# Wide values, a closing tile by halves, sample scaling in PSUM, and late forms behind the last row: five edits to a two-layer encoder kernel

## The chip, the cores and the metric

The kernel runs on one core of a Trainium2 chip. The metric is the device time of one execution in microseconds (us); lower is better. Before the change the median of three runs is 2803.09 us (2794.26 to 2809.61).

## The reference, cut to what matters

Two layers, each a token mixer (attention) and a channel mixer (a gated MLP with a convolution of width 3 over positions), for 1024 prompt tokens and 8 samples of 16 tokens, width 1024, 16 heads of 64, MLP width 2816, all in fp32. Every sub-layer is modulated by a condition c (one vector for the prompt, one for each sample) and closed by a layer norm:

```python
for l in range(2):
    sh_m, sc_m, g_m, sh_f, sc_f, g_f = split(silu(c) @ w_ada[l] + b_ada[l], 6)
    h = x * (1 + sc_m) + sh_m
    if l == 0:                       # mixer A: window of 3 chunks, 4 K/V heads
        q, k, v = split(h @ w_qkv_a)
    else:                            # mixer B: band of 9 chunks, 16 K/V heads
        q = h @ w_q_b                # k_b, v_b: see below
    mix = attention(q, k, v) @ w_o
    x = layer_norm(ALPHA * x + (1 + g_m) * mix, ln_g[l, 0], ln_b[l, 0])
    h = x * (1 + sc_f) + sh_f
    a, g = split(causal_conv3(h @ w_up[l]), 2)
    x = layer_norm(ALPHA * x + (1 + g_f) * ((gelu(g) * a) @ w_down[l]), ln_g[l, 1], ln_b[l, 1])
    if l == 0:                       # one K/V for mixer B, from its own modulation
        sh_kv, sc_kv = split(silu(c) @ w_ada_kv + b_ada_kv, 2)
        k_b, v_b = split((x * (1 + sc_kv) + sh_kv) @ w_kv_b, 2)
return x, ...                        # and the new K, V and convolution rows
```

## The kernel before, in words

The tokens lie in nine tiles of 128: tiles 0 to 7 are the prompt, tile 8 holds the samples. A tile's modulated rows stand transposed in H (`H[:, t, part, chunk, :]`). Every matrix is split into a high and a low part (`split`: a cast, L165, on ScalarE, and a subtraction, L176, on DVE or POOL), and each product is three matmuls, low x high, high x low, high x high. `wload` brings a piece of weights through a staging buffer `ws` (DMA issued by SP, L180) and splits it into a pair of slots, `wh` and `wl`.

Each layer goes through `attention`, `out_proj`, `up_phase` and `down_phase`. The code is written as one stream, and a scheduler that simulates the program's time on each engine sets the order of each engine's instructions; dependencies between tiles of memory are found by it, and `issue_after` adds a constraint by hand (what stands inside it comes after the named instruction).

- In layer 1's `attention`, K and V for mixer B are projected first. `vproj` takes V in four quarters of 256 columns: per quarter 9 tiles, per tile 24 matmuls (`mmX`, L395), whose result ScalarE casts (L444), DVE subtracts (L445) and SP stores as `vH` (L446); half of the tiles are copied by ScalarE once more for the output (L450). Quarter 0 comes before K (`kproj`, L383, with `rescale` on POOL), quarters 1 to 3 behind it. Then `qload(0)` brings the first block of query weights, and `load_hm` reloads the nine tiles that modulate into H for the queries (from `hmD`), modulates them (L907 on ScalarE; tile 8 by `sample_affine`) and splits them. H of a tile is free for this when V's last matmul on that tile has run.
- `sample_affine` scales and shifts tile 8, where each sample has its own vectors: per chunk of 128 columns one multiplication (L1006) and one addition (L1007) on DVE.
- `out_proj` computes per tile two halves of 512 columns into PSUM (`product`), multiplies by the gate in PSUM (L1045), adds the residual (L1046; `lasthalf` keeps the last of these), and `norm_tail` does the layer norm (L940 statistics, L971 normalisation), transposes on TensorE (L977) and modulates (L989 on ScalarE; tile 8 by `sample_affine`). Then `forms` builds sums and differences of blocks of the result, which the up-projection multiplies in seven products (P1 to P7) instead of eight. Forms are built for two token halves, q = 0 and q = 1. Those of q = 1 are the late forms: apart from P1 and P2 they are ordered after `lasthalf`.
- `up_phase` runs the seven products of both halves (L1225), with copies out of PSUM (L1243, L1254) and additions on DVE.
- `down_phase` takes three groups of three tiles (matmuls L1376, two halves `hf` for each tile). A tile's result is multiplied by the gate (`drain`, L1390) and, in layer 1, summed with the residual (L1401, with the row's sum accumulated) and normed by `norm_last`, which for tiles in VT takes two DVE operations (L958, L959) and for others ScalarE, POOL and DVE (L962 to L964), and is stored (L965). The last tile of the program is tile 8, not in VT.

Of the kernel before, what the change touches and what calls it, by code (L numbers as in the profile page):

```python
# [19 lines left out]
NFF = 22  # L20
# [73 lines left out]
class Trunk:  # L94
# [334 lines left out]

    def vproj(self, l, q, banks, tmp):  # L430
        nc = self.nc
        w = [self.wload(self.I[("wv0", "wv1")[l]][q, i], el="pv"[l == 0]) for i in range(2)]
        o0 = (896, 512)[l]
        cs = slice(q * 256, q * 256 + 256)
        for t in LV:
            ps = self.bank(banks.next())
            self.mmX(ps, t * 128, w, 4, 256)
            hl, v = tmp.next()
            v = v[:, 0:256]
            ts = slice(t * 128, t * 128 + 128)  # L440
            if t < 8:
                h4 = hl[:, 0:512].rearrange("p (h i d) -> p h i d", i=2, d=64)
                p3 = ps[:, 0:256].rearrange("p (h d) -> p h d", d=64)
                nc.scalar.copy(h4[:, :, 0, :], p3)  # L444
                nc.vector.tensor_sub(h4[:, :, 1, :], p3, h4[:, :, 0, :].bitcast(F32))  # L445
                nc.sync.dma_start(  # L446
                    self.vH[l][ts, 4 * q : 4 * q + 4, :], hl[:, 0:512].bitcast(F32).rearrange("p (h d) -> p h d", d=128)
                )
            if t * 128 >= o0:
                nc.scalar.copy(v, ps[:, 0:256])  # L450
                nc.sync.dma_start(self.O[("va", "vb")[l]][t * 128 - o0 : t * 128 - o0 + 128, cs], v)
            if t == 8:
                nc.sync.dma_start(self.vS[l][:, cs], v)


    def attention(self, l, wk):
# [67 lines left out]
        with ExitStack() as es:  # L524
            if l == 0:
                es.enter_context(self.tc.issue_after(self.lastx))
            self.vproj(l, 0, kvb, kvt)
        if l == 0:
            self.skew(0)
        else:  # L530
            zr = ka.ring(2, 1024)
            for c in range(8):
                self.kproj(1, c, self.wload(I["wk1"][c]), kvb, kvt)
                self.rescale(c, zr)
            self.rescale(8, zr)
            for q in range(1, 4):
                self.vproj(1, q, kvb, kvt)
            self.wring = Ring(self.wslots[0:2])
            qload(0)
            self.load_hm(Ring([pall[:, i * 1024 : i * 1024 + 1024] for i in range(3)]), self.affine(4, (8, 9), 1))  # L540
# [357 lines left out]
    def load_hm(self, ring, aff):  # L898
        nc, lead = self.nc, self.lastact
        G, B = aff  # L900
        for t in range(NT):
# [3 lines left out]
            if t < 8:  # L905
                for c in range(8):
                    nc.scalar.activation(s3[:, c, :], s3[:, c, :], AF.Identity, bias=B[:, c, 0:1], scale=G[:, c, 0:1])  # L907
            else:
                self.sample_affine(s3, s3, G, B, 0, 8, "v")
            with ExitStack() as es:  # L910
# [25 lines left out]
    def stats(self, x):  # L936
# [9 lines left out]
        return mv[:, 0:1], r  # L946

    def norm_last(self, t, x, s, ydst, junk):

# [17 lines left out]
    def norm_tail(self, t, x, xdst, aff, tb, h3, save=False):  # L967

        nc = self.nc
        mean, r = self.stats(x)  # L970
        nc.vector.tensor_scalar(x, x, mean, r, op0=ALU.subtract, op1=ALU.mult)  # L971
        sl = slice(t * 128, t * 128 + 128)
        G, B = aff
        for hf in range(2):
# [23 lines left out]

    def sample_affine(self, dst, src, G, B, c0, nc_, e):
        E = self.eng(e)  # L1000
        d4 = dst.rearrange("p c (s q) -> p c s q", q=16)
        s4 = src.rearrange("p c (s q) -> p c s q", q=16)
        for c in range(nc_):
            g = G[:, c0 + c, 1:9].unsqueeze(2).to_broadcast([128, 8, 16])
            b = B[:, c0 + c, 1:9].unsqueeze(2).to_broadcast([128, 8, 16])
            E.tensor_mul(d4[:, c], s4[:, c], g)  # L1006
            E.tensor_add(d4[:, c], d4[:, c], b)  # L1007

# [6 lines left out]
    def out_proj(self, l, xsrc, xdst, aff):  # L1015
# [26 lines left out]
        def add(t, x, hf, ps):  # L1042
            cs = slice(hf * 512, hf * 512 + 512)
            gate = self.gateP if t < 8 else self.gateS
            nc.vector.tensor_mul(ps, ps, gate[:, cs])  # L1045
            st = nc.vector.scalar_tensor_tensor(x[:, cs], x[:, cs], ALPHA, ps, op0=ALU.mult, op1=ALU.add)  # L1046
            self.lasthalf = st.ins

# [105 lines left out]
    def forms(self, q, hb, e, i):  # L1154
# [196 lines left out]
    def down_phase(self, l, xsrc, xdst, affs):  # L1351
# [19 lines left out]

        def mm(w, h, t, i, j):
            for hf in range(2):
                ps = self.bank(2 * i + hf)
# [61 lines left out]
        for g, ts in enumerate(GRP):  # L1436
# [16 lines left out]
            wh = [load(g, j) for j in range(NFF - nt, NFF)]  # L1453
            for i, t in enumerate(ts):
                for k, (w, h) in enumerate(wh):
                    mm(w, h, t, i, NFF - nt + k)
                row = rows.next()
                drain(i, t, row)
# [82 lines left out]
def layout(x):  # L1541
# [36 lines left out]
    z["wk1"] = cols(g["w_kv_b"][:, :D])  # L1578
    z["wv1"] = quarters(g["w_kv_b"][:, D:])
    z["wq1"] = cols(g["w_q_b"][0])  # L1580
# [58 lines left out]
```

## Time and profile before

| what | us |
|---|---|
| median of 3 runs | 2803.09 |
| the profiled execution | 2800.65 |
| its span in the trace | 2798.5 |
| TensorE matmuls busy | 2700.2 (96%) |
| DVE busy | 1665.2 (60%) |
| ScalarE busy | 1408.9 (50%) |
| POOL busy | 1056.7 (38%) |

The granted TensorE clock is 0.988 over the whole span. A matmul's busy time is modelled and includes its drain, so the 96% is a measure of how seldom TensorE waits, not of its rate. With so little waiting, an edit can act in two ways: it makes a stretch of matmuls itself shorter, or it shortens one of the few stretches in which TensorE stands. These are read from busy times by stage.

### The profile page before, as it was taken

The page shows a single profiled execution, that of the slowest core. Times are in us where ns is not written, and L with a number is a line of the kernel's source. Part 1 is how long each engine was busy: PE and PEld are TensorE (multiplying, and loading weights), DVE is VectorE, ACT ScalarE, POOL GpSimd, SP SyncE. Part 2 cuts the span into 40 slices and gives each one's busy share as a digit, 9 for nine tenths or more (in the row PEclk, how much of TensorE's full clock was granted, in tenths as well). Part 3 has the DMA queues.
Part 4 walks back from the last instruction along what each step waited for, and adds up shares of the span by engine and source line. Part 5 has one row for each costly group of instructions (what it writes and reads, how often), then busy time and mean ns, then how long its engine had stood idle before and what let it go on. Part 6 is the DMA issues. An engine that isn't in the chain of part 4 may idle for free.

```text
span 2798.5 us, 48858 instructions
## 1 busy us (share of the span) xinstructions
PE 2700.2 (96%) x18086; PEld 2415.9 (86%) x18086; DVE 1665.2 (60%) x3830; ACT 1408.9 (50%) x3012; POOL 1056.7 (38%) x1086
## 2 busy tenths in 40 slices
PE   8999889999999999999999999989899999999998
PEld 5887768999999998888999888867799999998886
DVE  4465757765555566766212677775966555567774
ACT  3465744544444444545425666662555445555441
POOL 1122337676566630001541121141877666640000
PEclk9999999999999999999999999999999999999999
DMA  9655443244444457865975456684222222238661
GB/s 331 193 155 164 124 140 113 97 139 138 155 134 128 146 158 266 310 215 182 303 249 177 113 150 185 168 250 132 99 89 74 78 83 75 76 104 290 232 209 71
DMA packets 215870, 454.47 MB, mean 162 GB/s; under 512 B 39280, under 2 KB 115264, under 8 KB 215632
## 3 DMA queue, kind: packets, MB, share of 16 engines
q1 hardware_dynamic: 215632, 451.35, 50.1%
q8 instruction: 143, 2.34, 0.3%
q14 instruction: 95, 0.78, 0.1%
HBM read 359.40 MB, written 101.30 MB: 165 GB/s over the span
## 4 chain that ended last, share of the span: by engine, by line
PE 77%; DVE 8%; DMA 7%; issue 4%; ACT 3%; POOL 1%; SPq 1%; POOLq 0%; ACTq 0%; DVEq 0%
PE PS L1225 34%; PE PS L1376 17%; PE PS L383 9%; PE PS L395 7%; DMA F<-in_adaw_dram 3%; PE PS L678 2%; PE PS L318 2%; PE PS L659 2%; PE PS L633 1%; DMA ws<-in_wo_dram 1%; DVE F L599 1%; PE PS L636 1%; DVE x1att L176 1%; PE PS L977 1%; PE PS L799 1%
## 5 line engine op out<-in xcount | busy, mean ns | idle before, releaser
L176 POOL TENSOR_TENSOR wl<-ws,wh 128x512 fp32r<-128x512 f32 (+1 forms) x217 | 324.2, 1497 | 649.3 <-ACT wh L165 628.3
L1279 DVE SCALAR_TENSOR_TENSOR PS<-F,PS 128x512 f32<-128x512 f32 (+2 forms) x704 | 349.1, 516 | 143.5 <-ACT PS L1286 63.6
L165 ACT CAST wh<-ws 128x512 fp32r<-128x512 f32 (+1 forms) x321 | 245.2, 769 | 313.6 <-PE PS L1376 99.3
L1225 PE MATMUL PS<-HX,wh 128*128 128x288 f32 x2616 | 401.0, 297 | 0.0
L1225 PEld LDWEIGHTS PS<-HX,wh 128*128 128x128 f32 x2616 | 364.4, 189 | 8.2 <-issue 8.2
L1376 PE MATMUL PS<-wh,HX 128*128 128x512 f32 x1164 | 361.7, 389 | 0.8 <-DVE HX L176 0.8
L1376 PEld LDWEIGHTS PS<-wh,HX 128*128 128x128 f32 x1164 | 218.4, 188 | 46.1 <-DVE HX L176 1.3
L1225 PE MATMUL PS<-HX,wl 128*128 128x288 f32 x1536 | 254.6, 297 | 0.2 <-ACT F L1254 0.2
L383 PE MATMUL PS<-HX,wh 128*128 128x384 f32 x1248 | 245.9, 340 | 0.0
L1376 PE MATMUL PS<-wl,HX 128*128 128x512 f32 x582 | 226.7, 390 | 0.6 <-DVE wl L176 0.6
L1225 PEld LDWEIGHTS PS<-HX,wl 128*128 128x128 f32 x1536 | 220.5, 189 | 7.1 <-issue 5.8
L383 PEld LDWEIGHTS PS<-HX,wh 128*128 128x128 f32 x1248 | 217.3, 189 | 5.4 <-issue 3.1
L1225 PE MATMUL PS<-x1att,wh 128*128 128x288 f32 x1168 | 181.9, 298 | 2.9 <-DVE x1att L176 1.3
L1286 ACT ACTIVATE PS<-F 128x512 f32<-128x512 f32 x176 | 138.1, 785 | 76.3 <-DVE F L1258 64.9
L1225 PEld LDWEIGHTS PS<-x1att,wh 128*128 128x128 f32 x1168 | 163.9, 189 | 8.9 <-issue 4.9
L395 PE MATMUL PS<-wh,HX 128*128 128x256 f32 (+1 forms) x936 | 168.4, 310 | 0.8 <-DVE C L599 0.8
L165 ACT CAST HX<-F 128x384 fp32r<-128x384 f32 (+3 forms) x232 | 136.6, 605 | 62.7 <-PE PS L1376 10.2
L717 POOL TENSOR_TENSOR F<-F,gatt 64x512 f32<-64x512 f32 x62 | 79.5, 1282 | 234.8 <-DVE F L690 181.5
L176 DVE TENSOR_TENSOR HX<-F,HX 128x384 fp32r<-128x384 f32 (+2 forms) x188 | 133.3, 719 | 37.2 <-ACT HX L165 33.6
L1376 PE MATMUL PS<-HX 128*128 128x512 f32 x630 | 145.1, 389 | 0.0
L395 PEld LDWEIGHTS PS<-wh,HX 128*128 128x128 f32 x936 | 133.8, 191 | 10.3 <-issue 1.5
L383 PE MATMUL PS<-HX,wl 128*128 128x384 f32 x624 | 130.3, 348 | 10.1 <-DVE HX L167 4.8
(244 smaller groups left out, 5486.2 us busy)
## 6 DMA issues: line engine op xcount, KB each, us to landing
F<-in_adaw_dram SPq DMA_DIRECT2D x112, 512.0 KB
ws<-in_wup_dram SPq DMA_DIRECT2D x92, 512.0 KB
ws<-in_wdn_dram SPq DMA_DIRECT2D x88, 512.0 KB
actD<-F SPq DMA_DIRECT2D x44, 576.0 KB
F<-actD SPq DMA_DIRECT2D x132, 192.0 KB
F<-in_wdn_dram SPq DMA_DIRECT2D x44, 512.0 KB
x1att<-kH SPq DMA_DIRECT2D x60, 256.0 KB
xd<-F SPq DMA_DIRECT2D x27, 512.0 KB
```

Source lines behind the costliest of these rows:

```text
L165: self.lastact = nc.scalar.copy(out, in_).ins
L176: self.eng(el).tensor_sub(lo, src, hi.bitcast(F32))
L318: mm = nc.tensor.matmul(ps[32 * j : 32 * j + 32, hf * 256 : hf * 256 + 256], self.cT[:, k * 32 : k * 32 + 32], w[n][:, j * 256 : j * 256 + ...
L383: self.nc.tensor.matmul(out, w[a][:, k * 128 : k * 128 + 128], self.Hx(p, k, s0, n), start=i == 0, stop=i == 23)
L395: self.nc.tensor.matmul(out[:, 0:n], H[:, t0 // 128, p, j * kn + k, :], w[a][:, k * n : k * n + n], start=i == 0, stop=i == 23,)
L659: nc.tensor.transpose(t[:, m * 128 : m * 128 + 128], p[:, (kt - k0) * 128 : (kt - k0) * 128 + 128], self.ident)
L678: nc.tensor.matmul(ob[:, i0 * 128 : i0 * 128 + w], vst[a][:, kt, :], pp[:, m1 : m1 + w], start=cnt == 0, stop=cnt == 2 * len(order) - 1, s ...
L717: self.eng("v" if last else "p").tensor_mul(on[r, q], on[r, q], rb[r, :])
L1225: nc.tensor.matmul(out, w[f][a][:, k * 128 : k * 128 + 128], x[:, k, :], start=start and i == 0, stop=i == 11, skip_group_check=True,)
L1279: nc.vector.scalar_tensor_tensor(o, v, w(i), o, op0=ALU.mult, op1=ALU.add)
L1286: nc.scalar.activation(yp, u[:, bl, 2:258], AF.Identity, bias=w(3), scale=w(2))
L1376: nc.tensor.matmul(ps, h[p][:, i * 128 : i * 128 + 128], w[q][:, hf * 512 : hf * 512 + 512], start=j == 0 and k == 0, stop=j == NFF - 1 an ...
```

## The change

Five things are done.

1. `vproj` takes its source, first column, width and destination as arguments. In layer 1, quarters 0 and 1 stay; columns 512 to 1023 are one half, 9 x 24 matmuls of 512 columns, with weights from a new array `wv1h` (four pieces of 128x1024). The weights of quarter 1 and of the half go to spare places in X1 and to weight slots 2 and 3, not through the ring `wring`; the half's evacuation ring has three buffers.
2. `sample_affine` is two operations per call over all its chunks: in `out_proj` a multiplication in place in PSUM and an addition from PSUM to SBUF, each 128x512; elsewhere the product goes to the destination first, as before.
3. The late forms are ordered after `lastnorm`, the normalisation of the last tile (L971, L1000 after), in place of `lasthalf`.
4. The program's last tile goes through a new function `close`: all matmuls of half 0, then all of half 1, with the gate's multiplication and the sum per half; the row's sum is put together; the Square on ScalarE runs beside the first closing operation on DVE; the second one and the store are done per half.
5. With these, the scheduler's order changes.

```diff
-    def vproj(self, l, q, banks, tmp):
+    def vproj(self, l, src, c0, n, banks, tmp, dst=None):
         nc = self.nc
-        w = [self.wload(self.I[("wv0", "wv1")[l]][q, i], el="pv"[l == 0]) for i in range(2)]
+        kn = 1024 // n
+        w = [self.wload(src[i], el="vp"[l], dst=dst and dst[i]) for i in range(8 // kn)]
...
-            self.mmX(ps, t * 128, w, 4, 256)
+            self.mmX(ps, t * 128, w, kn, n)
...
-            for q in range(1, 4):
-                self.vproj(1, q, kvb, kvt)
+            vt = [(self.X2[:, i * 1024 : i * 1024 + 1024], self.F[:, i * 512 : i * 512 + 512]) for i in range(3)]
+            spare = [tuple(self.X1[:, o + i : o + i + 1024] for i in (0, 1024)) for o in (0, 2048, 5120, 7168)]
+            spare += [self.wslots[2], (self.wslots[3][0], self.X1[:, 4096:5120])]
+            self.vproj(1, I["wv1"][1], 256, 256, kvb, kvt, spare[0:2])
+            self.vproj(1, I["wv1h"], 512, 512, kvb, Ring(vt), spare[2:6])
             self.wring = Ring(self.wslots[0:2])
             qload(0)
...
+    def close(self, t, row, x, ydst, product, junk):
+        nc = self.nc
+        part, rr = self.sm.next(), self.sm.next()
+        s, v, r = part[:, 0:1], rr[:, 0:1], rr[:, 1:2]
+        halves = [slice(hf * 512, hf * 512 + 512) for hf in range(2)]
+        for hf, n in enumerate(halves):
+            ps = product(hf)
+            nc.vector.tensor_mul(row[:, n], ps, self.gateS[:, n])
+            nc.vector.tensor_tensor_reduce(
+                out=row[:, n],
+                in0=row[:, n],
+                in1=x[:, n],
+                scale=1.0,
+                scalar=0.0,
+                op0=ALU.add,
+                op1=ALU.add,
+                accum_out=part[:, hf : hf + 1],
+            )
+        nc.vector.tensor_scalar(s, s, part[:, 1:2], -1.0 / D, op0=ALU.add, op1=ALU.mult)
+        nc.scalar.activation(junk, row, AF.Square, bias=s, accum_out=v)
+        nc.vector.scalar_tensor_tensor(x, row, s, self.lng, op0=ALU.add, op1=ALU.mult)
+        nc.vector.tensor_scalar(v, v, 1.0 / D, EPS, op0=ALU.mult, op1=ALU.add)
+        self.rsqrt(r, v)
+        for n in halves:
+            nc.vector.scalar_tensor_tensor(x[:, n], x[:, n], r, self.lnb[:, n], op0=ALU.mult, op1=ALU.add)
+            nc.sync.dma_start(ydst[t * 128 : t * 128 + 128, n], x[:, n])
...
-        nc.vector.tensor_scalar(x, x, mean, r, op0=ALU.subtract, op1=ALU.mult)
+        self.lastnorm = nc.vector.tensor_scalar(x, x, mean, r, op0=ALU.subtract, op1=ALU.mult).ins
...
-                self.sample_affine(h3[:, hf * 4 : hf * 4 + 4, :], self.tiles(ps), G, B, hf * 4, 4, "v")
+                self.sample_affine(h3[:, hf * 4 : hf * 4 + 4, :], self.tiles(ps), G, B, hf * 4, 4, not save)
...
-    def sample_affine(self, dst, src, G, B, c0, nc_, e):
-        E = self.eng(e)
+    def sample_affine(self, dst, src, G, B, c0, nc_, own=None):
+        n = [128, nc_, 8, 16]
         d4 = dst.rearrange("p c (s q) -> p c s q", q=16)
         s4 = src.rearrange("p c (s q) -> p c s q", q=16)
-        for c in range(nc_):
-            g = G[:, c0 + c, 1:9].unsqueeze(2).to_broadcast([128, 8, 16])
-            b = B[:, c0 + c, 1:9].unsqueeze(2).to_broadcast([128, 8, 16])
-            E.tensor_mul(d4[:, c], s4[:, c], g)
-            E.tensor_add(d4[:, c], d4[:, c], b)
+        g, b = (t[:, c0 : c0 + nc_, 1:9].unsqueeze(3).to_broadcast(n) for t in (G, B))
+        mid = s4 if own else d4
+        self.nc.vector.tensor_mul(mid, s4, g)
+        self.nc.vector.tensor_add(d4, mid, b)
...
             if q:
-                es.enter_context(self.tc.issue_after(self.lasthalf))
+                es.enter_context(self.tc.issue_after(self.lastnorm))
             put(P3, b22)
...
+                if last and final and i == 2:
+
+                    def product(hf):
+                        for k, (w, h) in enumerate(wh):
+                            mm(w, h, t, i, NFF - nt + k, (hf,))
+                        return self.bank(2 * i + hf)
+
+                    self.close(t, row, xs[i], xdst, product, tmp)
+                    continue
```

The order of ScalarE where V ends and attention of layer 1 begins, before (`wh<-ws` are casts of query weights, `HX<-F` of reloaded tiles, L590 is attention's first copy out of PSUM):

```order
L907 ACTIVATE F<-F,C 128x128 x4
L165 CAST wh<-ws 128x1024
L165 CAST HX<-F 128x1024 x2
L450 COPY F<-PS 128x256
L444 CAST HX<-PS 128x4x64
L165 CAST wh<-ws 128x1024
L165 CAST HX<-F 128x1024
L450 COPY F<-PS 128x256
L907 ACTIVATE F<-F,C 128x128 x8
L165 CAST HX<-F 128x1024
L590 ACTIVATE x1att_12291<-PS 64x384 x3
```

The same place after (L909 is L907 before, L445 is L444, L449 is L450, L592 is L590):

```order
L909 ACTIVATE F<-F,C 128x128 x8
L449 COPY F<-PS 128x512
L445 CAST HX<-PS 128x8x64
L165 CAST HX<-F 128x1024
L449 COPY F<-PS 128x512
L165 CAST HX<-F 128x1024
L445 CAST HX<-PS 128x8x64
L165 CAST HX<-F 128x1024
L449 COPY F<-PS 128x512
L592 ACTIVATE x1att_12267<-PS 64x384 x4
```

The casts of weights have gone from this place; on the same engine after, where K's last copies (L423) and quarter 1 of V (L445) meet, stand the casts of the first two blocks of query weights (the two `wh<-ws` rows):

```order
L165 CAST wh<-ws 128x1024
L423 COPY F<-PS 128x384
L445 CAST HX<-PS 128x4x64 x2
L165 CAST wh<-ws 128x1024
L445 CAST HX<-PS 128x4x64
```

They stand ahead of V's half now; before, they stood between V's last tiles. DVE at the end of layer 1's output projection, before (L1178 and L1179 are additions in `forms`, L176 the low parts, L940, L942 and L944 the last tile's norm):

```order
L1046 SCALAR_TENSOR_TENSOR F<-F,PS 128x512
L176 TENSOR_TENSOR x1att_12291<-F,x1att_12291 128x4x128
L1178 TENSOR_TENSOR F<-F 128x512
L176 TENSOR_TENSOR x1att_12291<-F,x1att_12291 128x4x32
L1178 TENSOR_TENSOR F<-F 128x4x32
L940 BN_STATS C<-F 128x6
L1179 TENSOR_TENSOR F<-F 128x512
L1179 TENSOR_TENSOR F<-F 128x4x32
L176 TENSOR_TENSOR HX<-F,HX 128x4x128
L942 BN_AGGR C<-C 128x2
```

The same place after (L1074 is L1046, L1205 is L1178):

```order
L1074 SCALAR_TENSOR_TENSOR F<-F,PS 128x512
L942 BN_STATS C<-F 128x6
L944 BN_AGGR C<-C 128x2
L946 TENSOR_SCALAR C<-C 128x1
L932 RECIPROCAL C<-C 128x1
L934 TENSOR_SCALAR C<-C 128x1
L935 TENSOR_SCALAR C<-C 128x1
L936 TENSOR_TENSOR C<-C 128x1
L1000 TENSOR_SCALAR F<-F,C 128x1024
L176 TENSOR_TENSOR x1att_12267<-F,x1att_12267 128x4x128
L1205 TENSOR_TENSOR F<-F 128x512
```

The last tile's norm runs through without a form between its rows. DVE at the program's end, before:

```order
L1390 TENSOR_TENSOR x1dn_24135<-PS,x1dn_24135 128x512 x2
L1401 ISA x1dn_24135,C<-x1dn_24135 128x1024
L1401 ISA C 128x1
L951 TENSOR_SCALAR C<-C 128x1
L955 TENSOR_SCALAR C<-C 128x1
L930 RECIPROCAL C<-C 128x1
L932 TENSOR_SCALAR C<-C 128x1
L933 TENSOR_SCALAR C<-C 128x1
L934 TENSOR_TENSOR C<-C 128x1
L961 TENSOR_TENSOR C<-C 128x1
L964 TENSOR_TENSOR x1dn_24135<-x1dn_24135,F 128x1024
```

And after, from the second half's multiplication on:

```order
L957 TENSOR_TENSOR x1dn_23834<-PS,x1dn_23834 128x512
L958 ISA x1dn_23834,C<-x1dn_23834 128x512
L958 ISA C 128x1
L968 TENSOR_SCALAR C<-C 128x1
L970 SCALAR_TENSOR_TENSOR x1dn_23834<-x1dn_23834,C,F 128x1024
L971 TENSOR_SCALAR C<-C 128x1
L932 RECIPROCAL C<-C 128x1
L934 TENSOR_SCALAR C<-C 128x1
L935 TENSOR_SCALAR C<-C 128x1
L936 TENSOR_TENSOR C<-C 128x1
L974 SCALAR_TENSOR_TENSOR x1dn_23834<-x1dn_23834,C,F 128x512 x2
```

The first half's pair (L957, L958) stands further up, between rows of the tile before; behind the second half's pair no other engine stands between DVE's rows but ScalarE's Square and root.

More of the change, by code (lines that the diff above doesn't have):

```diff
@@ L428, in kproj @@
                 nc.sync.dma_start(self.kS[l][rows, :], t[:, m:n])
[L430 removed]
+    def vproj(self, l, src, c0, n, banks, tmp, dst=None):
         nc = self.nc
[L432 removed]
+        kn = 1024 // n
+        w = [self.wload(src[i], el="vp"[l], dst=dst and dst[i]) for i in range(8 // kn)]
         o0 = (896, 512)[l]
[L434 removed]
+        cs, hs = slice(c0, c0 + n), slice(c0 // 64, (c0 + n) // 64)
         for t in LV:
             ps = self.bank(banks.next())
[L437 removed]
+            self.mmX(ps, t * 128, w, kn, n)
             hl, v = tmp.next()
[L439 removed]
+            hl, v = hl[:, 0 : 2 * n], v[:, 0:n]
             ts = slice(t * 128, t * 128 + 128)
             if t < 8:
[L442 to L443 removed]
+                h4 = hl.rearrange("p (h i d) -> p h i d", i=2, d=64)
+                p3 = ps[:, 0:n].rearrange("p (h d) -> p h d", d=64)
                 nc.scalar.copy(h4[:, :, 0, :], p3)
                 nc.vector.tensor_sub(h4[:, :, 1, :], p3, h4[:, :, 0, :].bitcast(F32))
[L446 to L448 removed]
+                nc.sync.dma_start(self.vH[l][ts, hs, :], hl.bitcast(F32).rearrange("p (h d) -> p h d", d=128))
             if t * 128 >= o0:
[L450 removed]
+                nc.scalar.copy(v, ps[:, 0:n])
                 nc.sync.dma_start(self.O[("va", "vb")[l]][t * 128 - o0 : t * 128 - o0 + 128, cs], v)
@@ L908, in load_hm @@
             else:
-                self.sample_affine(s3, s3, G, B, 0, 8, "v")
+                self.sample_affine(s3, s3, G, B, 0, 8)
             with ExitStack() as es:
@@ L1045, in add @@
             nc.vector.tensor_mul(ps, ps, gate[:, cs])
-            st = nc.vector.scalar_tensor_tensor(x[:, cs], x[:, cs], ALPHA, ps, op0=ALU.mult, op1=ALU.add)
-            self.lasthalf = st.ins
+            nc.vector.scalar_tensor_tensor(x[:, cs], x[:, cs], ALPHA, ps, op0=ALU.mult, op1=ALU.add)
         def half(t, x, hf):
@@ L1370, in down_phase, with mm @@
         aff = None
-        def mm(w, h, t, i, j):
-            for hf in range(2):
+        def mm(w, h, t, i, j, hs=(0, 1)):
+            for hf in hs:
                 ps = self.bank(2 * i + hf)
@@ L1454, in down_phase @@
             for i, t in enumerate(ts):
+                row = rows.next()
+                if last and final and i == 2:
[5 more added lines that the diff above has]
+                    continue
                 for k, (w, h) in enumerate(wh):
                     mm(w, h, t, i, NFF - nt + k)
-                row = rows.next()
                 drain(i, t, row)
@@ L1578, in layout @@
     z["wk1"] = cols(g["w_kv_b"][:, :D])
-    z["wv1"] = quarters(g["w_kv_b"][:, D:])
+    z["wv1"] = quarters(g["w_kv_b"][:, D : D + 512])
+    z["wv1h"] = halves(g["w_kv_b"][:, D:])[1]
     z["wq1"] = cols(g["w_q_b"][0])
```

2 lines of the change are left out of this document (1 added, 1 removed).

## The prediction

> **What bounds the kernel now.** I read the page first, then a table by stage, then what TensorE waits for in those stages, then single rows.
>
> ```profile
> span 2798.5 us, 48858 instructions
> PE 2700.2 (96%) x18086; PEld 2415.9 (86%) x18086; DVE 1665.2 (60%) x3830; ACT 1408.9 (50%) x3012; POOL 1056.7 (38%) x1086
> PE 77%; DVE 8%; DMA 7%; issue 4%; ACT 3%; POOL 1%; SPq 1%; POOLq 0%; ACTq 0%; DVEq 0%
> ```
>
> TensorE is busy for 2700.2 of 2798.5 us, so all its idle time together is 98.3 us, and no edit beside the matmuls can win more than the idle time (and the slow clock after it) of its own stage. The stages that the change touches, with the busy time of PE, PEld, DVE, ACT and POOL, then the granted clock, the DMA share and GB/s:
>
> ```profile
> 440.00:545.00 105.00, 100.71 (x597) 88.97 (x597) 79.25 (x144) 55.08 (x130) 81.13 (x80) 0.98 0.27 94
> 1310.00:1345.00 35.00, 33.14 (x232) 31.02 (x231) 27.11 (x60) 19.32 (x45) 7.78 (x5) 1.00 0.50 185
> 1345.00:1440.00 95.00, 95.00 (x573) 95.00 (x572) 12.86 (x24) 32.10 (x66) 66.71 (x36) 1.00 0.92 307
> 1510.00:1560.00 50.00, 41.69 (x260) 40.01 (x259) 26.16 (x59) 38.47 (x86) 8.20 (x3) 0.90 0.46 150
> 1960.00:2010.00 50.00, 47.59 (x224) 38.87 (x223) 43.22 (x82) 28.64 (x75) 48.42 (x43) 0.97 0.33 117
> 2010.00:2030.00 20.00, 14.05 (x86) 12.89 (x85) 18.81 (x30) 9.99 (x27) 13.46 (x13) 0.83 0.17 57
> 2784.00:2798.50 14.50, 0.90 (x4) 0.40 (x3) 5.05 (x12) 2.68 (x4) 2.34 (x1) 0.71 0.12 50
> ```
>
> What is there to win is read from these rows as idle time plus (1 - clock) x busy time. Output projection to up-projection of layer 0 (440 to 545): 4.29 + 2.0 = 6.3 us. End of layer 0, the first quarter of V (1310 to 1345): 1.9. The K projection of layer 1 (1345 to 1440): nothing, TensorE never stops, but DMA runs at a share of 0.92. V to attention (1510 to 1560): 8.31 + 4.2 = 12.5. Output projection to up-projection of layer 1 (1960 to 2030): 2.41 + 1.4 and 5.95 + 2.4, together 12.2. The tail (2784 on): 13.6, one tile's norm with nothing beside it. TensorE's waits there, the first two in 1500 to 1560, the next two in 1960 to 2075, the last in 440 to 545 (total, times, longest):
>
> ```profile
> PE PS L633 <- DVE x1att L591: 4.1, 2, 3.9
> PE PS L383 <- POOL wl L176: 3.9, 1, 3.9
> PE PS L1225 <- ACT F L1243: 3.1, 1, 3.1
> PE PS L977 <- DVE F L971: 2.4, 1, 2.4
> PE PS L1225 <- ACT F L1243: 2.6, 1, 2.6
> ```
>
> **The change part by part.** A, the closing tile. Its rows before (start, duration):
>
> ```profile
> 2784.51 0.39 PE L1376 MATMUL PS<-wh,HX 128*128 128x512 f32 x1
> 2784.26 1.37 DVE L1390 TENSOR_TENSOR x1dn<-PS,x1dn 128x512 f32<-128x512 f32 x2 [1.89 <-PE PS L1376]
> 2785.66 1.23 DVE L1401 CUSTOM_DVE_ANT_0 x1dn<-x1dn 128x1024 f32<-128x1024 f32 x1
> 2787.18 1.15 ACT L954 ACTIVATE x1dn<-x1dn,C 128x1024 f32<-128x1024 f32 x1 [7.85 <-DVE C L951]
> 2789.57 0.16 DVE L934 TENSOR_TENSOR C<-C 128x1 f32<-128x1 f32 x1
> 2790.02 1.24 ACT L962 ACTIVATE x1dn<-x1dn,C 128x1024 f32<-128x1024 f32 x1 [1.18 <-DVE C L961]
> 2791.34 2.34 POOL L963 TENSOR_TENSOR x1dn<-x1dn,F 128x1024 f32<-128x1024 f32 x1 [61.34 <-ACT x1dn L962]
> 2793.71 1.23 DVE L964 TENSOR_TENSOR x1dn<-x1dn,F 128x1024 f32<-128x1024 f32 x1 [3.79 <-POOL x1dn L963]
> ```
> ```profile
> L958 DVE SCALAR_TENSOR_TENSOR x1dn<-x1dn,C,F x4: 1275/1276/1276, 2613.6 to 2779.0; 128x1024 f32<-128x1024 f32 x4
> ```
>
> The matmuls are the same, only the first half's now all come first, so its multiplication and sum lie beside the second half's matmuls. After the last matmul stand: the second half's multiplication (half of L1390's 1.37), which ends at 2785.63 as before; a sum over 512 columns, half of L1401's 1.23 and some issue, to 2786.4; one small operation to add the two sums (0.16 by L934, and a hop to ScalarE), to 2786.65; then the same run from L954's start at 2787.18 to L934's end at 2789.73, 2.55 us, so to 2789.2. The first product of the closing formula (a 1024-wide operation like L958, 1.28) lies beside L954's Square, 1.15 and its accumulator. Then two halves of the last operation at 0.64 to 0.69 each: 2790.6, where before L962, L963 and L964 end at 2794.94. That is 4.3. The last transfer is half as large; from 2794.94 to the span's end at 2798.5 are 3.56 us, of which I take 0.6 (between 0 and half, 1.8, for want of a row for the smaller transfer in an idle queue). A = -4.9, bounds -4.3 and -6.1.
>
> B, the matmuls of V's last 512 columns, 2 x 9 x 24 = 432 of 256 columns, become 9 x 24 = 216 of 512. Chain rows with long unbroken runs, V at 256, the output projection at 512 and the down-projection at 512:
>
> ```profile
> 1449.33 59.00 PE PS L395 x492
> 1932.63 21.72 PE PS L395 x94
> 1059.80 97.77 PE PS L1376 x430
> ```
>
> These are 119.9, 231.1 and 227.4 ns each. 432 x 0.1199 = 51.8; 216 x 0.2311 = 49.9, or 49.1 at the down-projection's rate. B = -1.9 (same line of code), bounds -1.0 (should weights arrive less smoothly) and -2.7. By the rows a matmul costs 2 x 119.9 - 231.1 = 8.7 ns beside its columns. The Trainium skill (TensorE: Matmul & The Clock Gate, "Wait — 56ns, not 53.3ns?") gives only about 2.5 ns fixed per matmul at full clock, measured back to back; by it the merge would be worth 216 x 2.5 ns = 0.5 us, and B an estimate of -0.5. The rows here disagree, in a stream with a weight load before every matmul, and I go by the rows.
>
> C, what stands around V. First pieces of the chain at its end and, for the full clock, a run of L383 from before V; then two rows of TensorE:
>
> ```profile
> 1439.97 9.36 PE PS L383 x54
> ...
> 1527.54 0.93 ACT wh L165
> ...
> 1533.15 6.73 DMA F<-hmD
> ...
> 1547.20 2.56 PE PS L383 x8
> ```
> ```profile
> 1530.96 2.93 PE L383 MATMUL PS<-HX,wl 128*128 128x384 f32 x8 [3.88 <-POOL wl L176]
> 1544.86 0.47 PE L633 MATMUL PS<-x1att 128*128 128x128 f32 x1 [3.89 <-DVE x1att L591]
> ```
>
> Before, V ends at 1527, and only then the query weights are cast (L165, behind the layer's modulations L907 on ScalarE), so TensorE waits 3.88; the last of the nine reloads hmD lands at 1539.9, DVE scales it in 16 operations, and TensorE waits another 3.89 for attention's first DVE result. After each wait it restarts at 320 ns a matmul in place of 9.36 / 54 = 173, 1.2 us per eight. In the new order the query weights' casts stand ahead of V (ScalarE and SP), and a tile of H comes free every 24 x 0.2311 = 5.5 us of V's half rather than every 24 x 0.1199 = 2.9 us of the last quarter, so reloads and modulations go in step with V (ScalarE has then eight L907s, a cast and an evacuation or two to do in 5.5 us). The first wait and its restart should go (5.1). The second, 3.89 + 1.2, I halve: attention's first results still come after V, but the sample tile's 16 operations become 2. With what is left of the slow clock, C = -8.0, bounds 0 and -12.5. Beside it 18 narrow evacuations (ScalarE, DVE, SP) become 9 wide ones, none on the path. V's ring has 3 buffers for 4, and each is needed again after 3 x 5.5 = 16.6 us, against 6.73 us for a 512 KB transfer (hmD's): covered, and uncovered only by stores of 2.5 times that length. The weights' new places cost nothing by themselves; the loads of K and V for the first heads that used these places come later, and V's 50 us hide them.
>
> D, sample scaling and late forms. DVE's rows in layer 1's output projection, and all of L1006 and L1007 in the program (min/median/max, first and last start):
>
> ```profile
> 1981.98 1.67 DVE L1006 TENSOR_TENSOR F<-PS,C 128x128 f32<-128x128 f32 x8
> 1983.57 0.36 DVE L1007 TENSOR_TENSOR F<-F,C 128x128 f32<-128x128 f32 x1
> 1984.45 8.57 DVE L1007 TENSOR_TENSOR F<-F,C 128x128 f32<-128x128 f32 x7
> 1994.08 0.69 DVE L1045 TENSOR_TENSOR PS<-PS,F 128x512 f32<-128x512 f32 x1
> ```
> ```profile
> L1006 DVE TENSOR_TENSOR F<-PS,C x24: 275/281/293, 455.5 to 1983.4; 128x128 f32<-128x128 f32 x24
> L1007 DVE TENSOR_TENSOR F<-F,C x32: 276/286/1382, 456.3 to 1991.6; 128x128 f32<-128x128 f32 x32
> ```
>
> Beside a busy POOL the additions with both operands in SBUF take up to 1382 ns, the multiplications out of PSUM at most 293. The new four operations are 128x512, each with one operand in PSUM: 0.69 by L1045, 2.8 in all, where layer 1 had 1.67 + 0.36 + 8.57 = 10.6. DVE gains 7.8 us there, and in layer 0, whose POOL is as busy, something like it. Of this the path gets only the wait that it sets: in layer 1 L977 <- L971, 2.4 and the slow clock behind it.
>
> Late forms: before, DVE's forms of the second token half stand inside the last tile's norm; now the norm's twelve rows come first. L1243's wait is for a ScalarE copy queued behind a form's cast that waits for DVE; with the norm's row first, the 3.1 (layer 1) and 2.6 (layer 0) should go, but the forms start later by what the norm's end needs. In layer 1 I take 2.4 + 1.0 (clock) + 3.1 = -6.5, bounds -2.4 (the forms give back the rest) and -12.2 (all that the two stages lose); in layer 0 half of the 2.6 and a third of its slow clock, -2.0, bounds +1 (the forms late by more than the wait that goes) and -6.3.
>
> The sample tile at the end of layer 0 gets the two-operation scaling too, with its sum in SBUF; the stage (1310 to 1345) loses 1.9 in all, so between 0 and -1.9, and I take 0, since what its waits are for I can't tell from that row.
>
> Sum: -4.9 - 1.9 - 8.0 - 6.5 - 2.0 = -23.3. The profiled execution took 2800.65 us (span 2798.5), 2.4 below the median of 2803.09; 2800.65 - 23.3 = 2777.3, **2777**.
>
> **The rivals.** R1, the handover keeps its waits: the last tile of H is still reloaded after V's last matmul, at 6.73 us for the transfer, and attention's first DVE operations come behind it. Then C = 0: 2785. For it: 3.9 of the 8.3 idle are such a wait. Against: two of three steps ahead of it have moved.
>
> R2, the late forms give D back: now all behind the norm, they are F<-F operations with two SBUF operands, L1007's kind, beside a POOL that is busy 13.46 of 20 us. D = 0 but for L977's wait in layer 1 (2.4): 2800.65 - 4.9 - 1.9 - 8.0 - 2.4 = 2783. For it: of the 5.95 that 2010 to 2030 loses, 2.8 are other waits than L1243's, so that the next ones stand close behind. Against: DVE has 7.8 us less to do before the forms. The Trainium skill (GPSIMD Engine Reference, "8. Key points") says that GpSimd shares its SBUF interfaces with VectorE and collides with VectorE instructions that have two SBUF inputs: by that rule the forms stay slow wherever POOL works, and the scaling out of PSUM does not, as L1006 and L1007 show.
>
> R3, the other side: K starves. Four 512 KB pieces of V's weights and up to four of the queries' now pass SP's queue, and most of them ScalarE and POOL too, while K runs with DMA at 0.92. At 307 GB/s eight pieces are 4.2 MB, 13.7 us; with all of them ahead of K's own weights, and a restart of 1.2 after each, TensorE loses up to 23, and nothing is left of C: 2800.65 - 15.3 + 23 = 2808, slower than before. Against: K's own loads stand ahead of V's in SP's order, and eight loads of K and V for the first heads leave the stage. It decides from about 15 us of waits of L383 in 1345 to 1440.
>
> **How the numbers follow.** Forecast 0.57 (2768 to 2783), R1 0.16, R2 0.15, R3 0.06, something else in the rebuilt order of the rest (attention, up-phase) 0.06. A difference under 0.5%, 14 us, can't be told from none by a measurement of this kernel. The forecast and most of R2, with half of R1, lie beyond it: faster 0.76; the rest of R1 and R2 and half of R3 make same 0.19; slower 0.05. The sum of all lower bounds is 2800.65 - 39.8 = 2761, which would need every one at once; R1 and R2 together give 2791. The range 2765 to 2795 leaves out those ends and R3.
>
> **What would show it.** A: no POOL row behind the last matmul, and 10 us from it to the end for 14. B: long runs of L395 at 231 ns in V. C: no wait for POOL's wl at V's end, PE busy over 47 of 50 around it; and L383 without a wait in K (else R3). D: the four scaling operations at 0.69 each beside a busy POOL; no wait of L977's successor for the norm, no 3 us wait for the first copy of the up-projection. Wrong would be: a wait of the forms' consumers (x1att, HX from L176) that grows by what these lose.

## The result, and the profile after

The changed kernel takes 2782.02 us (median of 6 runs, 2777.44 to 2787.97), the kernel before 2801.62 (6 runs). The ratio is 0.9925, interval 0.9904 to 0.9945. The forecast was 2777 (2765 to 2795) and faster; both came. The profiled span goes from 2798.5 to 2775.3 us, 23.2 less.

Where they lie is read from the start of the first and the end of the last TensorE row of each stage (for the output projection, to the first row of the up-projection). Each kernel was profiled twice, so every stage also has its scatter:

| stage (us) | before, two profiles | after, two profiles |
|---|---|---|
| start to layer 0's output projection | 364.3, 364.7 | 360.7, 362.4 |
| layer 0's output projection and up-projection | 678.4, 679.0 | 679.5, 679.7 |
| V of layer 1 behind K | 77.9, 77.9 | 75.6, 75.6 |
| V's first matmul to the 569th of the query projection's 576 | 364.1, 363.7 | 351.0, 351.1 |
| V's end to layer 1's output projection | 358.7, 356.8 | 348.9, 347.3 |
| layer 1's output projection | 123.8, 122.2 | 119.7, 119.6 |
| its up-projection | 505.2, 507.1 | 505.1, 504.7 |
| last matmul to the end | 13.6, 13.6 | 8.8, 8.9 |

The expectations below call the 569th matmul the 576th; the last one ends 2.5 us later in every kernel, so the differences are the same. Both down-projections (275.8 and 270.2) and K stay within 0.4. The stage table of the forecast, with windows moved along with their stages (busy PE, PEld, DVE, ACT, POOL, then clock, DMA share, GB/s):

```profile
436.40:541.40 105.00, 99.70 (x594) 87.67 (x593) 70.75 (x129) 54.39 (x130) 83.56 (x79) 1.00 0.29 98
1343.00:1438.00 95.00, 95.00 (x572) 95.00 (x571) 12.27 (x24) 32.39 (x67) 70.81 (x35) 1.00 0.88 295
1505.40:1555.40 50.00, 48.30 (x262) 43.10 (x261) 25.86 (x57) 32.35 (x68) 2.36 (x1) 1.00 0.44 148
1945.70:1991.60 45.90, 45.90 (x224) 37.76 (x223) 35.85 (x68) 28.11 (x74) 44.20 (x39) 1.00 0.37 127
1991.60:2011.60 20.00, 13.39 (x82) 12.06 (x81) 19.31 (x32) 14.05 (x39) 16.58 (x18) 0.85 0.21 79
2766.10:2775.30 9.20, 0.37 (x2) 0.00 (x0) 5.21 (x12) 1.45 (x3) 0.00 (x0) 0.71 0.25 97
```

K (1343) is as full as before and DMA no busier: R3 did not come. V to attention (1505) loses 1.7 us where it lost 8.3, at full clock. The last part of layer 1's output projection (1945) has no gap at all. But the 20 us behind it (1991) have 13.39 of work at a clock of 0.85, where before they had 14.05 at 0.83: nothing was won there. TensorE's waits in 1955 to 2070 say what stands in place of L1243's 3.1 and L971's 2.4:

```profile
PE PS L1252 <- DVE x1att L176: 3.9, 1, 3.9
PE PS L1006 <- DVE F L1000: 2.2, 1, 2.2
```

The handover in the chain (V's matmuls, then 72 matmuls of the query projection back to back), and the tail's rows:

```profile
1504.84 17.67 PE PS L395 x76
1522.51 12.51 PE PS L383 x72
```
```profile
2766.09 0.39 PE L1403 MATMUL PS<-wh,HX 128*128 128x512 f32 x1
2766.51 0.69 DVE L957 TENSOR_TENSOR x1dn<-PS,x1dn 128x512 f32<-128x512 f32 x1 [1.63 <-PE PS L1403]
2767.24 0.69 DVE L958 CUSTOM_DVE_ANT_0 x1dn<-x1dn 128x512 f32<-128x512 f32 x1
2768.22 1.28 DVE L970 SCALAR_TENSOR_TENSOR x1dn<-x1dn,C,F 128x1024 f32<-128x1024 f32 x1
2768.28 1.15 ACT L969 ACTIVATE x1dn<-x1dn,C 128x1024 f32<-128x1024 f32 x1 [7.38 <-DVE C L968]
2770.87 1.41 DVE L974 SCALAR_TENSOR_TENSOR x1dn<-x1dn,C,F 128x512 f32<-128x512 f32 x2
```

From the last matmul's start to the last DVE result are 6.2 us, before 10.4 (2784.51 to 2794.94), and from there to the end 3.0, before 3.6, with a transfer half as large.

### The profile page after: what moved, and what is told of

Its sections match the earlier page's. It is cut to its first block, busy times and chain, and to the rows that moved or that the text cites. A ratio compares the mean times of both kernels' runs of the same rounds, so it can differ in the third digit from the quotient of the medians.

```text
span 2775.3 us, 48313 instructions
## 1 busy us (share of the span) xinstructions
PE 2689.8 (97%) x17870; PEld 2397.7 (86%) x17870; DVE 1645.9 (59%) x3775; ACT 1407.3 (51%) x2998; POOL 1057.6 (38%) x1085
## 4 chain that ended last, share of the span: by engine, by line
PE 82%; DMA 6%; DVE 6%; POOL 2%; ACT 2%; issue 2%; SPq 0%; DVEq 0%; POOLq 0%; ACTq 0%
PE PS L1252 34%; PE PS L1403 19%; PE PS L383 10%; PE PS L395 8%; PE PS L680 2%; DMA F<-in_adaw_dram 2%; PE PS L661 2%; PE PS L318 2%; DMA ws<-in_wo_dram 1%; PE PS L635 1%; DVE F L601 1%; PE PS L638 1%; POOL HX L176 1%; PE PS L801 1%; DVE HX L667 0%
## 5 line engine op out<-in xcount | busy, mean ns | idle before, releaser
L176 POOL TENSOR_TENSOR wl<-ws,wh 128x512 fp32r<-128x512 f32 (+1 forms) x212 | 309.5, 1463 | 632.7 <-ACT wh L165 602.9
L1403 PEld LDWEIGHTS PS<-wh,HX 128*128 128x128 f32 x1164 | 218.4, 188 | 46.4 <-DVE HX L176 1.3
L395 PE MATMUL PS<-x1att,HX 128*128 128x512 f32 (+1 forms) x846 | 188.2, 368 | 3.7 <-ACT x1att L165 2.6
L395 PEld LDWEIGHTS PS<-x1att,HX 128*128 128x128 f32 x846 | 142.1, 188 | 32.1 <-ACT x1att L165 3.2
L176 DVE TENSOR_TENSOR HX<-F,HX 128x384 fp32r<-128x384 f32 (+3 forms) x188 | 129.6, 700 | 31.6 <-ACT HX L165 30.4
L1403 PEld LDWEIGHTS PS<-HX 128*128 128x128 f32 x630 | 118.2, 188 | 24.6
```

The costliest lines, as they stand in the source:

```text
L176: self.eng(el).tensor_sub(lo, src, hi.bitcast(F32))
L395: self.nc.tensor.matmul(out[:, 0:n], H[:, t0 // 128, p, j * kn + k, :], w[a][:, k * n : k * n + n], start=i == 0, stop=i == 23,)
L1403: nc.tensor.matmul(ps, h[p][:, i * 128 : i * 128 + 128], w[q][:, hf * 512 : hf * 512 + 512], start=j == 0 and k == 0, stop=j == NFF - 1 an ...
```

## The experiments

Each kernel below is the changed one with the edit shown; ratios are to the kernel before.

**Scatter.** Both kernels once more, unaltered.

> The changed kernel once more, unaltered, for the scatter of a stage from one execution to the next. In the first profile layer 0's attention ended 3.55 us earlier than before the change, though TensorE's rows have the same order up to there. Theory 'chance': the start of layer 0's output projection lies between 361 and 365 us here (360.7 before), i.e. not reliably at 360.7. Rival 'an effect of the change': it lies within 0.5 us of 360.7. Both expect the stages named in the forecast to repeat: V's last matmul to the first of layer 1's output projection 348.9 within 2 us, output projection 119.7 within 1 us, last matmul to end 8.8 within 0.3 us.

> The kernel before the change once more, unaltered, for the scatter of its stages. Theory 'the 3.5 us ahead of layer 0's output projection are chance': that projection starts anywhere between 359 and 367 us (the seven profiles of kernels with the change gave 359.4 to 366.4, the first profile before it 364.3). Rival: it starts within 0.5 us of 364.3. Both expect the stages that the change touches to repeat: V and attention up to the 576th matmul of the query projection 364.1 within 0.5, output projection and up-projection of layer 1 together 628.9 within 1, last matmul to end 13.6 within 0.1.

Measured: spans 2774.8 and 2798.2, stages as in the table. Layer 0's output projection began at 362.4 and 364.7. The second lies within the rival's 0.5 us, but two profiles prove little: kernels with the change began it anywhere from 358.9 to 367.6 us, though TensorE's order up to there is that of before in all of them. So the first profile's 3.5 us are not counted as a gain. The samples' part of attention moves like this in both layers: by 8.7 us ahead of layer 0's output projection, and by 5.3 between the 569th query matmul and layer 1's (70.5 to 75.8), over all profiles. One such place, in the kernel named late_old below (a TensorE row and a window):

```profile
394.28 0.88 PE L395 MATMUL PS<-x1att,HX 128*128 128x512 f32 x2 [2.70 <-ACT x1att L165]
```
```profile
358.00:440.00 82.00, 75.98 (x416) 57.81 (x415) 48.13 (x126) 32.66 (x80) 20.82 (x14) 0.90 0.43 139
```

A wait of 2.70 us stands there with a clock of 0.90 over the whole window (1.00 in the changed kernel's first profile). The edits are therefore judged by the stages without such a part, which repeat to 0.1 to 0.6 us in the changed kernel, more than by spans.

**The tail.**

```diff
-                if last and final and i == 2:
+                if False:
```

> The changed kernel with the last tile closed as before the change (both halves' matmuls interleaved, one norm of 1024 columns through ScalarE, POOL and DVE). Theory 'the tail is its own stage': last matmul to the span's end goes from 8.8 back to 13.6 us, everything ahead is unmoved, the span is longer by 4.8. Rival 'the scheduler arranges the last group otherwise': the tail is 13.6 but the last group's matmuls end at another time by more than 2 us, so that the span moves by less than 3 or more than 7.

Measured: ratio 0.9945 (0.9927 to 0.9964), span 2781.1, last matmul to end 13.5; every other stage is within 1.5 us of the changed kernel's first profile, layer 1's down-projection unmoved at 270.2. The theory holds: of the 5.8 us that the span is longer, 4.7 are the tail's.

**V: width and places.** v_old puts quarters 1 to 3 back through the ring; v_narrow uses the spare places for three narrow quarters; wide_ring keeps the wide half but gives no places:

```diff
# v_old
+            for q in range(1, 4):
+                self.vproj(1, I["wv1"][q], q * 256, 256, kvb, kvt)
# v_narrow
+            for q in range(1, 4):
+                self.vproj(1, I["wv1"][q], q * 256, 256, kvb, kvt, spare[2 * q - 2 : 2 * q])
# wide_ring
+            self.vproj(1, I["wv1"][1], 256, 256, kvb, kvt)
+            self.vproj(1, I["wv1h"], 512, 512, kvb, Ring(vt))
```

> The changed kernel with V of layer 1 in quarters through the weight ring again, as before the change; scaling, forms and tail stay changed. Theory 'the query weights and reloads that moved ahead carry the handover': V takes 77.9 us in place of 75.6, TensorE waits about 4 us for POOL's low part of the query weights behind V's last matmul and 2 to 4 us for attention's first results, and V's end to the output projection takes 356 to 359 in place of 347.3 to 349.6; the span is longer by 10 to 12. Rival 'the sample tile's two operations in place of sixteen carry half of it': the first wait comes back but not the second, and that stage takes 352 to 355, the span longer by 6 to 8.

> The changed kernel with V's columns 512 to 1023 in two quarters of 256, but with their weights in the spare places (so that the weight ring is free for the query weights as early as in the changed kernel). Theory 'places, not width': V takes 77.9 us (the width's 2.3 lost), no wait for the query weights behind V, and V's end to the output projection stays at 347 to 351; the span is longer by 2 to 4. Rival 'width gives the reloads their time': H's tiles come free 2.9 us apart in place of 5.5, the reloads end after V, attention's first results are late by 3 to 6 us, that stage takes 352 to 356, the span longer by 6 to 9.

> The changed kernel with V's last 512 columns in one wide half, but its weights and those of quarter 1 through the weight ring, so that the query weights come as late as before: the width without the places. From V's first matmul to the 576th of the query projection the kernels took 351.1 (both), 355.8 (places alone) and 361.6 (neither). Theory 'the two add up': 361.6 - 4.7 = 356.9, within 1. Rival 'the query weights are the last to come, whatever V's width': the wait for their low part stays near 4 us and only V's own rate is won, 359 to 361.

| us | neither (v_old) | places alone | width alone | both |
|---|---|---|---|---|
| V behind K | 77.9 | 76.3 | 75.1 | 75.6 |
| of it, quarter 1 (216 matmuls) | 25.91 | 25.20 | 25.91 | 25.20 |
| of it, columns 512 to 1023 | 52.00 | 51.10 | 49.15 | 50.38 |
| V's first matmul to the 410th of TensorE behind V | 153.8 | 148.0 | 147.6 | 143.2, 143.2 |
| V's first matmul to the 569th of the queries | 361.6 | 355.8 | 358.7 | 351.0, 351.1 |
| ratio of the times | 0.9959 (0.9944 to 0.9973) | 0.9955 (0.9938 to 0.9971) | 0.9955 (0.9938 to 0.9972) | 0.9925 |

TensorE's rows behind V in v_old, v_narrow and wide_ring:

```profile
1534.09 2.93 PE L383 MATMUL PS<-HX,wl 128*128 128x384 f32 x8 [3.81 <-POOL wl L176]
1547.73 2.93 PE L383 MATMUL PS<-HX,wl 128*128 128x384 f32 x8 [3.70 <-ACT HX L165]
```
```profile
1547.23 0.48 PE L634 MATMUL PS<-x1att 128*128 128x128 f32 x1 [3.29 <-DVE x1att L592]
```
```profile
1534.45 1.87 PE L383 MATMUL PS<-HX,wl 128*128 128x384 f32 x8 [2.27 <-POOL wl L176]
1546.40 1.66 PE L383 MATMUL PS<-HX,wl 128*128 128x384 f32 x8 [1.61 <-ACT HX L165]
```

The places take away the wait for POOL's low part of the query weights. The width shortens both waits in the ring and, beside the places, takes away the one for attention's first results. At the 410th matmul of TensorE behind V all four kernels have run matmuls of the same kinds and numbers; further on wide_ring's order parts from the others'. Up to the 410th places alone win 5.8 us, width alone 6.2 (2.9 of them V's own rate) and both 10.6: each does over half, and they overlap. At the 569th query matmul width alone has only 2.9 left, and both seem to win 1.8 more than the sum. But from the 410th to the 1421st matmul, where the kinds and numbers agree again, the other kernels take 139.5 us and wide_ring 142.8: TensorE's order differs there, as by the 384th query matmul it has run 1171 in place of 1185. What the width is worth is therefore not to be read at the 569th.

The expectations fared so. v_old's theory held in its waits (the second came from a reloaded tile's cast), though its total (354.2 from V's end to the output projection) is the rival's number. v_narrow's 'places, not width' fell: V kept 1.6 of the 2.3, the width is worth 4.7 us beside the places, and the rival's stage of 352 to 356 came (355.3). For wide_ring neither held: the wait for the low part is 2.27, not near 4, and the 358.7 lies between the sum of 356.9 and the rival's 359 to 361.

V's own time has a term of its own: the rate of a matmul differs with the buffer that its weights come from. Quarter 1, the same 216 matmuls of 256 columns, in the chain of v_old and of the changed kernel:

```profile
1452.54 25.55 PE PS L395 x213
1447.09 24.97 PE PS L395 x214
```

These are 120.0 ns each with weights from the ring and 116.7 from the places in X1. In v_narrow the second quarter, in X1 too, runs at 116.7 and the last, in weight slots 2 and 3, at 119.9. The wide half goes the other way: 227 ns a matmul from the ring (49.15 us) and 233 from the spare places (50.38).

Beyond these, 2.2 to 2.5 us at the 569th matmul separate v_old from the kernel before, where the sample tile's scaling differs. In affine_old below, with V changed, the old scaling moves that matmul by 0.2 at most, so it can count only while the reloads are late; with the old V it was not tried alone.

**Sample scaling.** affine_old goes back to sixteen operations per tile; affine_sbuf writes the product to SBUF:

```diff
-        mid = s4 if own else d4
+        mid = d4
```

> The changed kernel with the samples scaled as before, sixteen operations of 128x128 per tile. Theory 'the scaling out of PSUM carries layer 1's gain': DVE's additions are stretched to 1.2 us again beside POOL, TensorE waits about 2.4 us more in layer 1's output projection, that projection takes 123 to 124 us in place of 119.7, and the span is longer by 3 to 5. Rival 'DVE has room': the additions are as slow as before but the projection stays within 1 us of 119.7, and the span within 1.5.

> The changed kernel with the samples' product written to SBUF, so that the addition has both operands there (two operations of 128x512 per half still). Theory 'two SBUF operands beside POOL': the addition takes 1.2 to 2.8 us in layer 1's output projection in place of 0.63, DVE loses 1 to 4 us there, the projection takes 120.5 to 123 in place of 119.7, and the stage up to the up-projection's end grows by 0 to 1.5, as with sixteen operations. Rival 'the number of operations is what counts': the additions take under 0.8 us and the projection stays within 0.4 of 119.7.

Rows of DVE: the changed kernel's additions (all of those out of PSUM), affine_old's, affine_sbuf's (min/median/max):

```profile
L1035 DVE TENSOR_TENSOR F<-PS,C x4: 672/680/682, 454.4 to 1970.5; 128x512 f32<-128x512 f32 x4
```
```profile
1974.60 8.58 DVE L1036 TENSOR_TENSOR F<-F,C 128x128 f32<-128x128 f32 x7
```
```profile
L1035 DVE TENSOR_TENSOR F<-F,C x7: 676/1505/1784, 457.5 to 1975.7; 128x512 f32<-128x512 f32 x6, 128x1024 f32<-128x1024 f32 x1
```

With both operands in SBUF the same addition takes up to 1784 ns beside POOL, out of PSUM never over 682. The Trainium skill (GPSIMD Engine Reference, "8. Key points") names two SBUF inputs of VectorE among what collides with GpSimd, and the rows agree. On the path this is worth little. In affine_old (ratio 0.9940, 0.9918 to 0.9961) layer 1's output projection is back at 123.6, but its up-projection is 2.7 shorter (502.4), so that the two together cost 1.1 to 1.7 more than in the changed kernel: the theory was right for the projection and wrong for the gain of the layer. In layer 0 the up-projection is 2.8 us longer (553.0). In affine_sbuf (0.9935, 0.9918 to 0.9953) the projection stays at 119.5: its theory was right on the operation, its rival on the path.

**Late forms.** late_old orders them after the last residual again:

```diff
-                es.enter_context(self.tc.issue_after(self.lastnorm))
+                es.enter_context(self.tc.issue_after(self.lasthalf))
```

> The changed kernel with the late forms ordered after the last residual again, as before the change. Theory 'the late forms only move the wait': TensorE waits again about 3 us for the first copy of the up-projection of layer 1, and the 3.9 us wait for a late form is gone or shorter; the stage from layer 1's output projection to the end of the up-projection is the same within 2 us (624.8 now), the span within 3 us. Rival 'the late forms carry layer 1's gain' (the forecast's own step): the stage is longer by 3 to 5 us and the span by 4 to 7.

Measured: ratio 0.9944 (0.9926 to 0.9962), span 2783.0. Layer 1's two stages take 628.5 in place of 624.3 to 624.8 (625.2 in undo_close), the up-projection 508.9. My theory, that the late forms only move a wait, falls; the rival, which was the forecast's own step, is right for layer 1. In layer 0 the up-projection takes 549.9, in the changed kernel 550.2 and 550.8: there the new order wins nothing. TensorE's rows in layer 1:

```profile
2003.23 0.78 PE L1253 MATMUL PS<-HX 128*128 128x288 f32 x4 [2.28 <-ACT F L1271]
2005.86 1.33 PE L1253 MATMUL PS<-x1att,wl 128*128 128x288 f32 x4 [1.84 <-ACT x1att L165]
2012.15 1.92 PE L1253 MATMUL PS<-x1att,wh 128*128 128x288 f32 x8 [3.05 <-DVE x1att L176]
```

Both waits stand there: the copy's and, behind it, the form's. With old forms the scaling is worth 0.4 in layer 1 (628.9 to 628.5), with new ones 1.1 (626.0 to 624.8); the new forms are worth 2.9 with the old scaling (628.9 to 626.0) and 3.7 with the new. The kernel before stands for both old here, though V and the tail differ in it too. A second profile of either kernel moves these by 0.3 to 0.5.

**What the late forms still cost.** In the changed kernel the chain behind the last row is this (two rows of DVE, one of TensorE):

```profile
2004.14 2.65 DVE L1206 TENSOR_TENSOR F<-F 128x512 f32<-128x512 f32 x2
2006.72 0.94 DVE L176 TENSOR_TENSOR x1att<-F,x1att 128x512 fp32r<-128x512 f32 x1
```
```profile
2007.71 2.29 PE L1252 MATMUL PS<-x1att,wh 128*128 128x288 f32 x8 [3.94 <-DVE x1att L176]
```

Two subtractions of 1.3 us each, where the same line takes 0.68 at 2009.79, while POOL stands idle, are ahead of the one low part that TensorE waits for. Two remedies: q0_first makes TensorE take the first token half's second unit first; late_p_first writes all late P1 and P2 first and orders the other late forms after them (`lastp`; `lastlo` is the last low part that `split` made), not after the norm:

```diff
# q0_first
-        unit(1, (1,), w1)
+        with self.tc.issue_after(q0):
+            unit(1, (1,), w1)
# late_p_first
         if q:
             put(P2, b21)
+            yield
...
-                es.enter_context(self.tc.issue_after(self.lastnorm))
+                es.enter_context(self.tc.issue_after(self.lastp))
...
+        self.lastp = self.lastlo
+        for f in self.late:
+            next(f)
```

> The changed kernel with one more constraint: the up-projection's first unit on the second token half (which reads the late forms) comes after the second unit on the first half. Theory 'TensorE waits for late forms because its order takes them too early': the 3.9 us wait for a late form in layer 1 and the 0.5 to 1.6 in layer 0 vanish, and output projection plus up-projection of layer 1 take 620.5 to 623 in place of 624.3 to 625.2; the span is shorter by 2 to 6. Rival 'the next thing is just as late': the forms' place is taken by waits for weights of the second unit (DMA, ScalarE, POOL), the stage stays within 1 us or is longer, the span within 2.

> The changed kernel with the late forms P1 and P2 of all three blocks written first and the other late forms ordered after them, not after the last row's norm. In the changed kernel the low part of the last block's P1 was ready to be computed at about 2005.5 us and stood behind two subtractions until 2006.7, while TensorE waited 3.9 us for it. Theory 'that place in DVE's order is worth its time': the wait is 1.5 to 3 us, and output projection plus up-projection of layer 1 take 622.5 to 624 in place of 624.3 to 625.2; layer 0 may gain as much. Rival 'the other forms are late next': the wait for the first is shorter and another of the same size stands within 30 us behind, the stage stays at 624 to 626.5.

> The kernel with the late P1 and P2 first once more, to see whether its gain over the changed kernel repeats. If it is the order's: output projection plus up-projection of layer 1 take 622 to 623 us (624.3 to 625.2 in the changed kernel), and layer 0's up-projection stage 546.3 to 547.5 (550.2 to 550.8), so about 5 us less in all; the span is 2770 to 2776 for whatever the samples' part of attention takes. If it was chance, one of the two stages lies at the changed kernel's value.

q0_first: ratio 0.9970 (0.9955 to 0.9984), slower than the changed kernel. Layer 1's up-projection takes 513.2 (8.1 more), layer 0's 554.5. The rival was right, and worse than it said: other waits came instead.

```profile
2012.92 0.80 PE L1252 MATMUL PS<-HX,wl 128*128 128x288 f32 x4 [2.45 <-ACT HX L165]
2024.08 0.91 PE L1252 MATMUL PS<-gup,wl 128*128 128x288 f32 x4 [3.28 <-DVE F L1282]
```

late_p_first: ratios 0.9913 (0.9890 to 0.9936) and, as best_again, 0.9906 (0.9889 to 0.9923), spans 2772.7 and 2767.5. Layer 1's two stages take 622.5 and 622.3, layer 0's up-projection 546.8 and 546.9 (changed kernel 550.2 and 550.8). Both repeat, together some 5 to 6 us, and the rival falls. best_again's span lies under the 2770 to 2776 foreseen; its layer 0 attention ended early, at 358.9. In layer 1 the 3.94 has become this:

```profile
2004.42 0.81 PE L1256 MATMUL PS<-x1att,wl 128*128 128x288 f32 x4 [0.90 <-ACT x1att L165]
```

By its medians (2778.64 and 2774.99 us) it is the fastest of these kernels. Its intervals overlap the changed kernel's 0.9904 to 0.9945, so it is the two stages that set them apart, not the ratio.

## Why the prediction was right, and where it was not

- **The tail** (-4.9): -4.8 in the table, -4.7 by undoing it. Every step came out as worked: L969 beside L970, no POOL row. (The "10 us from it to the end" among the prediction's signs does not follow from its own sum, which makes 8.7; measured are 8.8.)
- **V's matmuls** (-1.9): -2.3. The size was near by luck. The half itself won 1.6 (52.0 to 50.4), and 0.7 came from quarter 1, whose width did not change. The step that failed is "the weights' new places cost nothing by themselves": with them quarter 1 took 0.7 less and the half 1.2 more than from the ring (49.15 to 50.38). In the ring the merge is worth 2.9, in the places 0.7 (51.1 to 50.4), not the 1.9 by 8.7 ns a matmul. The Trainium skill's figure (TensorE: Matmul & The Clock Gate, "Wait — 56ns, not 53.3ns?") gives an estimate of 0.5 for 216 matmuls, which I had set aside. It is near the second and far from the first, and since the second compares matmuls of unequal rates (116.7 and 119.9 ns), neither settles it.
- **The handover** (-8.0): -10.3 to -10.8 beyond V's own 2.3 at the 569th query matmul (364.1, 363.7 to 351.0, 351.1), about -9.7 at the output projection. Both waits went, and the slow clock with them: the mechanism was right, and the term was too small because I had halved the second wait. R1 did not come.
- **Layer 1's output and up-projection** (-6.5): -4.1 to -5.0. L971's wait and the clock behind it went (the projection is 2.5 to 4.2 shorter), L1243's 3.1 went, and a 3.9 us wait for a late form and a 2.2 us wait for the last row's norm came. The step that failed is that the path gets the waits that go, for both edits at once; the sign named for it, a growing wait for x1att from L176, is the 3.9. The two edits also lean on each other, as the four combinations show.
- **Layer 0** (-2.0): none, +0.5 to +1.3 in the two stages. Half of the copy's 2.6 did go (1.2 are left, and the clock of the window is full), but in the first profile a wait for ScalarE's HX of 1.5 and one for DVE's of 1.6 stand behind it. The step that failed is the same: nothing was counted for what stands behind the wait.
- **R2** is nearer than the forecast for the late forms and the scaling in both layers together: it gave -2.4, the forecast -8.5, measured are -2.8 to -4.5. Its mechanism, late forms slow beside POOL, is what the 3.9 us wait shows.
- **The sum** (-23.3) agrees with the profiled -23.2 partly by chance: a handover larger than forecast makes up for part of the smaller gain in layers 0 and 1. The terms that the change explains come to about -4.8 - 2.3 - 9.7 - 4.5 + 1 = -20.3, and layer 0's attention, 2 to 4 us shorter here, is scatter. The medians' -19.6 fits the -20.3.

## What to carry to other kernels

Where TensorE is busy 97% of the time, a wait is removed only when what stands right behind it is ready too: look for the next consumer's chain and put its one operation first, as the late P1 shows, rather than delaying a whole group or reordering the consumer. Where weights for the next stage wait for a buffer ring, spare places and wider, slower steps in the stage before each help, and their gains overlap. Compare two kernels at a point up to which TensorE has run the same matmuls in both: a changed order further on can hide a gain or feign one. Judge edits worth a few us by stages that repeat to a fraction of that, not by the span.

## What the runs showed of the hardware that was not expected

- A 512-wide addition beside a busy POOL took up to 1784 ns with both operands in SBUF and 682 at most with one in PSUM, while in affine_sbuf the projection lost no time by it.
- A matmul of 256 columns in V took 120.0 ns with weights from the ring, 116.7 from X1 and 119.9 from weight slots 2 and 3; one of 512 columns took 227 ns from the ring and 233 from the spare places. The ring's rates stand in all profiles that use it, and those of the changed kernel's places in all nine that have them; the narrow quarters in other places and the wide half in the ring were profiled once each. The reason is open.
- In the changed kernel a 128x512 subtraction of two SBUF operands on DVE (L1206) took 1.3 us while POOL worked and 0.68 while it stood idle.
